# Reordering the chunked linear attention of a streaming-encoder layer, and moving left factors of its feed-forward behind a weight split

## Chip, cores and metric

The kernel runs on one core of a Trainium2 chip (trn2). The metric is the device time in microseconds (us) of one execution, the median of several runs. Beside the times there is one profiled execution, from which the views below are taken.

## What is computed

One layer of a hybrid encoder for 512 frames of width 1024: three parallel branches (gated linear attention over chunks of 64 frames, a causal attention with forget gates, a cross attention into 256 memory tokens), merged by gates, then a squared-ReLU feed-forward. The two places that the change touches are the linear attention and the feed-forward:

```python
def gla_chunk_causal(q, k, v, log_a):        # 4 heads, DK = 64, DV = 128, chunks of 64 frames
    b = cumsum(log_a within the chunk); b_last = b[:, :, -1:]
    q_pos = qc * exp(b)
    a_causal = einsum('bnthd,bnshd->bnhts', q_pos, kc * exp(-b))
    a_anti   = einsum('bnthd,bnshd->bnhts', qc * exp(-b), kc * exp(b))
    attn = where(lower, a_causal, a_anti)
    o_intra = einsum('bnhts,bnshv->bnthv', attn, vc)
    chunk_kv = einsum('bnshd,bnshv->bnhdv', kc * exp(b_last - b), vc)
    prev = scan(state * exp(b_last) + kv)     # the state before each chunk
    o_inter = einsum('bnthd,bnhdv->bnthv', q_pos, prev)
    return o_intra + o_inter
...
    o_gla = rmsnorm(o_gla, g_gla_head) * silu(gg)
...
    h = h + merged @ w_out
    u2 = rmsnorm(h, g_ffn)
    h = h + square(relu(u2 @ w_ff1)) @ w_ff2
    return rmsnorm(h, g_final)
```

## The kernel before

All matrix products with weights run in a split form: an operand is rounded to a high part (`hi`, a cast on ScalarE, ACT) and the rest is its low part (`lo`, a subtraction on VectorE, DVE). `mm3` (L170 to L172) issues three matmuls for one product: high by high and the two mixed ones. `split_w` (L160, L161) and `split_b` (L1331, L1333) make the parts of a weight block of 128 x 1024, `split` (L223, L224) those of an activation. Weight blocks come by DMA into a ring of three buffers, and their high and low parts have rings of three.

The order of the instructions of the TensorE (PE) is the order of the program text. The order of the other engines' instructions is drawn up by a scheduler when the kernel is built; `tc.issue_after(x)` puts what is written under it behind `x` on `x`'s engine, and `in_order()` keeps a stretch of DVE, ACT and SP instructions in the written order.

PSUM holds eight banks in two pools of four: `mmt()` (pool pmm, tiles "mm", used by the products with weights) and `at_()` (pool pa, tiles "a", used by attention, transposes and a part of the products). A tile gets a bank that has been read out.

**Linear attention.** Heads go in two pairs j = 0, 1; 512 frames are handled as four tiles of 128 (two chunks each). The steps of a pair are functions:

- `decays(j)`: cumulative sums of the log decays by matmul (L882), exponentials on ACT (L888, L891), scaled keys and queries `kn`, `qpos`, `kp`, `qneg` on DVE (L896 to L901).
- `key_turn(j)`: three transposes of `kn` (L908) and their copy.
- `gla_scores(j)`: 32 score matmuls (L941), 16 for each of the two masks, the two heads of the pair on the two halves of 64 rows; DVE copies the scores under the mask into `at` (L943), which GpSimd has cleared (L935). At its end it calls `states(j)`: 12 matmuls (L921) into one "mm" tile and the chain of states on DVE (L927, L928).
- `gla_values(j)`: 16 matmuls of scores by values (L952), 12 of queries by states (L956), then the root mean square (square on ACT L962, sum on DVE L963, root on GpSimd L230) and the scaling on DVE (L967).
- `gla_turn(h)`: four transposes (L973) of head h, the product with the gate on DVE (L975) and its split.

`u_sum(n)` are sums on DVE for a later stage, `gate_ready(b)` brings the first weights of that stage. `weave` puts these steps between the units of a filler stream: four projections `gla_g` and four `fox_late` gates, 64 units, each unit one step of the contraction (three matmuls of 512 columns), eight units to one "mm" tile. Each step has a share, and after step i the filler runs up to `units * sum(shares[:i + 1]) // sum(shares)`.

**Feed-forward.** Each of four quarters of the hidden width multiplies by `w_ff1` (first product) and by `w_ff2` (second product), each with seven products of sums of blocks in place of eight. `first_quarter` writes the order of the first quarter out by hand. At its end it issues the second product's parts 1, 2 and 5 (`second`), then the drain of part 2 into the residual (`evac`, L1327), two subtractions (`sub`, L1324) and the left factors of parts 7 (slot 1) and 4 (slot 2) by `left`. `second_product(0)` goes on with parts 3, 6, 7, 4: for each it makes the weight's parts with `split_b` and issues 24 matmuls. Part 3 reads the left factors of slot 0, part 6 those of slot 3.

Of the kernel before, what the change touches and what calls it, by code (L numbers as in the profile page):

```python
# [14 lines left out]
ALU = mybir.AluOpType  # L15
AX = mybir.AxisListType

P = 128
# [4 lines left out]
NT = S // P  # L23
# [40 lines left out]
def hybrid_block(ctx, tc, chunks, wst, memT, xT, xN, gffn, gfin, wup, cst, out):  # L64
    nc = tc.nc
# [5 lines left out]
    def nm(s):  # L71
        uid[0] += 1
        return f"{s}_{uid[0]}"
# [10 lines left out]
    def mmt(shape=None):  # L84
        return pmm.tile(shape or [P, 512], F32, tag="mm", name=nm("mm"))

    def at_(shape=None):
        return pa.tile(shape or [P, 512], F32, tag="a", name=nm("a"))

    def f(ap):  # L90
        return ap.bitcast(F32)
# [77 lines left out]
    def mm3(ps, lh, ll, rh, rl, start, stop, on=False):  # L169
        nc.tensor.matmul(ps, lh, rh, start=start, stop=False, skip_group_check=on)  # L170
        nc.tensor.matmul(ps, lh, rl, start=False, stop=False, skip_group_check=on)  # L171
        nc.tensor.matmul(ps, ll, rh, start=False, stop=stop, skip_group_check=on)  # L172
# [49 lines left out]
    def split(hi, lo, src):  # L222
        nc.scalar.copy(hi, src)  # L223
        return nc.vector.tensor_tensor(lo, src, f(hi), op=ALU.subtract).ins  # L224
# [41 lines left out]
    with pool("front") as fp:  # L266
# [33 lines left out]
        ps = at_()  # L300
# [14 lines left out]
        for j in range(4):  # L315
# [3 lines left out]
            for k in (2 * j, 2 * j + 1):  # L319
# [8 lines left out]
                else:  # L328
                    _, act, vec = parts.send((None, act, vec))
# [98 lines left out]
        ps = at_()  # L428
# [446 lines left out]
    with pool("gla") as lp:  # L875
# [36 lines left out]
        def states(j):  # L912


            dec, kt = gs["d", j][0], gs["k", j]
            mid = gs["s", j] = lp.tile([P, NT, P], F32, tag="mid", name=nm("mid"))
            pv = mmt([P, NT, P])
            for t in range(NT - 1):
                for e in range(2):
                    h = 2 * j + e  # L920
                    nc.tensor.matmul(pv[64 * e:64 * e + 64, t, :], kt[:, t, 64 * e:64 * e + 64], gv[:, t, h * P:(h + 1) * P],  # L921
                                     start=True, stop=True)
            for t in range(NT - 1):
                x = pv[:, t, :]
                if t:
                    x = mid[:, 0, :]
                    nc.vector.tensor_tensor(x, mid[:, t, :], pv[:, t, :], op=ALU.add)  # L927
                nc.vector.tensor_scalar(mid[:, t + 1, :], x, dec[:, t:t + 1], None, op0=ALU.mult)  # L928

        def gla_scores(j):  # L930

            _, kn, kp, qp, qn = gs["d", j]
            ats = gs["a", j] = [lp.tile([P, NT, P], F32, tag=f"at{e}", name=nm("at")) for e in range(2)]
            for at in ats:
                nc.gpsimd.memset(at, 0.0)  # L935
            for m, (kk, qq) in enumerate(((kn, qp), (kp, qn))):
                ps = [at_([P, NT, P]) for _ in range(2)]
                for t in range(NT):
                    sl = slice(t * P, (t + 1) * P)
                    for e in range(2):  # L940
                        nc.tensor.matmul(ps[e][:, t, :], kk[half[e], sl], qq[half[e], sl], start=True, stop=True)  # L941
                for e in range(2):
                    nc.vector.copy_predicated(ats[e], msk_s[:, m:m + 1, :].to_broadcast([P, NT, P]), ps[e])  # L943
            states(j)
# [51 lines left out]
        def gate_ready(b):  # L996
# [3 lines left out]
        A11, A12, A21, A22 = ([f(t[:, 4 * k:4 * k + 4, 256 * i:256 * i + 256]) for t in (uhi, ulo)] for i in range(2) for k in range(2))  # L1000

        steps = (
            (decays, (0,), 13), (key_turn, (0,), 5), (gla_scores, (0,), 8), (gla_values, (0,), 4), (decays, (1,), 5),
            (gla_turn, (0,), 0), (gla_turn, (1,), 4), (key_turn, (1,), 5), (gla_scores, (1,), 2), (u_sum, (1,), 6), (gla_values, (1,), 6),
            (u_sum, (3,), 0), (gla_turn, (2,), 3), (gate_ready, ("11",), 0), (gate_ready, ("21",), 0), (gla_turn, (3,), 3))
        weave([partial(fn, *a) for fn, a, _ in steps], 64, *[gla_g(j) for j in range(4)], fox_late(), shares=[n for *_, n in steps])
    gst.close()
# [24 lines left out]
    with pool("outp") as op_:  # L1032
# [236 lines left out]
        def first_mms(n, w, ps, go=None, low_last=False):  # L1269

            wh, wl = (t.rearrange("p (a k c) -> p a k c", a=2, k=4) for t in w)
            (uh, ul), s = U2[n]

            def mm(a, k, x, y, start, stop):
                nc.tensor.matmul(ps[:, a, :], x[:, a, k, :], y[:, s, k, :], start=start, stop=stop, skip_group_check=go is not None)  # L1275

            for low in range(1 + low_last):
                for a in range(2):
                    for k in range(4):
                        if not low:  # L1280
                            mm(a, k, wh, uh, k == 0 if go is None else go and a == k == 0, False)
                            mm(a, k, wh, ul, False, False)
                        if low or not low_last:
                            mm(a, k, wl, uh, False, k == 3 and (go is None or a == 1))
                        yield
# [9 lines left out]
        rest = first_mms(2, ws[1], banks[0][1], True)  # L1295
# [14 lines left out]
    with pool("ff") as yp:  # L1310
# [12 lines left out]
        def sub(to, x, y, op=ALU.subtract):  # L1323
            return nc.vector.tensor_tensor(to, x, y, op=op).ins  # L1324

        def add(to, x, op=ALU.add):
            return nc.vector.tensor_tensor(to, to, x, op=op).ins  # L1327

        def split_b(raw, after=None):
            hi, lo = (wp.tile([P, 1024], F32R, tag=g, name=nm(g)) for g in ("hi", "lo"))  # L1330
            nc.scalar.copy(hi, raw)  # L1331
            with tc.issue_after(after) if after is not None else ExitStack():
                nc.vector.tensor_tensor(lo, raw, f(hi), op=ALU.subtract)  # L1333
            return hi, lo

        load_n = [0]
# [15 lines left out]
        def left(i, slot, src):  # L1352
            split(ch[i][:, slot, :], cl[i][:, slot, :], src)
# [18 lines left out]
        def first_quarter():  # L1372
# [4 lines left out]
            o12, o22 = ([od[i][:, h, :] for i in range(2)] for h in range(2))  # L1377
# [30 lines left out]
            def left_low(i, slot, src):  # L1408
                nc.vector.tensor_tensor(cl[i][:, slot, :], src, f(ch[i][:, slot, :]), op=ALU.subtract)
# [10 lines left out]
            with tc.issue_after(norm_end[0]), tc.issue_after(norm_end[1]), in_order():  # L1420
# [133 lines left out]
                    second(5, i, five)  # L1554
                for i in range(2):
                    left_low(i, 0, o12[i])
                for t in range(2):
                    evac(0, 2, t, two[t])
                for i in range(2):
                    sub(o21[i], o11[i], o21[i])  # L1560
                    left(i, 1, o21[i])
            for i in range(2):
                left(i, 2, o22[i])

        def first_evac(n, i, ps):

# [37 lines left out]
        def evac(q, n, t, ps):  # L1604
            if n in (1, 2):
                add(C(0, 0, t), ps)
            if n == 3:
                add(C(0, 1, t), ps)
            if n == 6:
                add(C(0, 1, t), ps, ALU.subtract)  # L1610
                if q == 0:
                    nc.scalar.copy(R7[t], ps)
                else:
                    add(R7[t], ps)
            if n == 7:
                add(R7[t], ps)
            if n == 4:
                add(C(1, 0, t), ps)
# [19 lines left out]
        def second_mms(q, n, js, ps, w, ts=range(2), cols=slice(0, 512), fresh=None):  # L1638

            keep, on = n in (1, 5), q == NQ - 1 and n in CHAIN  # L1640
            first, end = fresh or (not (keep and q or on), not keep or q == NQ - 1)
            for t in ts:
                for i in js:
                    for k in range(2):
                        sl = slice(256 * k + t * P, 256 * k + t * P + P)
                        mm3(ps[t], ch[i][:, LEFT[n], sl], cl[i][:, LEFT[n], sl], w[i][0][:, k, cols], w[i][1][:, k, cols],
                            i == k == 0 and first, i == k == 1 and end, on and fresh is None)
                if q < NQ - 1 and js[-1] == 1 and not keep and (q or n != 2):
                    evac(q, n, t, ps[t])

        def second_product(q):
            for n in SECOND[0 if q else 3:]:
                ps = held[n] if n in (1, 5) else [mmt() for _ in range(2)]
                for i in range(2):
                    w = {i: [x.rearrange("p (k c) -> p k c", k=2) for x in split_b(factor_raw(q, n, i))]}
                    second_mms(q, n, [i], ps, w)
                for i in range(2):
                    if n == 1:
                        add(od[i][:, 0, :], s1[i])
                        left(i, 0, od[i][:, 0, :])  # L1660
                    if n == 2:
                        sub(ev[i][:, 1, :], ev[i][:, 0, :], ev[i][:, 1, :])
                        left(i, 1, ev[i][:, 1, :])
                    if n == 5:
                        left(i, 2, od[i][:, 1, :])

        def last_product():
# [64 lines left out]
            with in_order():  # L1732
# [115 lines left out]
                scale_r(2, 1, nc.sync)  # L1848
                scale_r(3, 1, nc.scalar)
                scale(3, 0, nc.sync, 256)  # L1850
        first_quarter()
        second_product(0)
        for q in range(1, NQ):
            first_product(q, 0)
            loads = load_blocks(q)
# [113 lines left out]
```

## Time and profile before

| | |
|---|---|
| median of 3 runs | 809.85 us (809.58 to 811.93) |
| profiled execution | 809.57 us |
| its span, first to last instruction | 807.8 us |
| PE busy | 798.7 us (99%) |
| DVE, ACT, GpSimd (POOL) busy | 595.6, 445.7, 108.0 us |
| mean granted TensorE clock | 0.997 |
| DMA | 161.29 MB, mean 200 GB/s |

Times in the views count from the start of the span. PE is the matmuls, PEld the weight loads that run beside them. In the timeline a row is start, duration, engine, line, operation, output<-inputs, shapes and count; equal neighbours are merged. In the chain a row is start, duration and the piece of work. The linear attention lies between 254 and 316 us, the part of the feed-forward that the change moves between 527 and 566 us.

### The profile page before, as it was taken

What the parts mean: (1) busy time and instruction counts of PE and PEld (TensorE: products, weight loads), DVE (VectorE), ACT (ScalarE), POOL (GpSimd) and SP (SyncE); (2) the same over time, 40 slices, a digit from 0 to 9 for tenths busy, and PEclk for the clock granted to TensorE, in tenths of its full rate; (3) what the DMA queues carried; (4) which work ended last, traced back from release to release, by engine and by line L of the source; (5) the groups of instructions that cost most, each with busy time, mean ns of one, the idle gap of its engine ahead of it and who ended that gap; (6) DMA issues with size and microseconds to landing.
All of it is one profiled execution on the core that took longest, in us unless ns stands there. A gap on an engine that the chain in (4) does not pass through costs nothing.

```text
span 807.8 us, 12486 instructions
## 1 busy us (share of the span) xinstructions
PE 798.7 (99%) x4799; PEld 704.8 (87%) x4799; DVE 595.6 (74%) x917; ACT 445.7 (55%) x702; POOL 108.0 (13%) x136
## 2 busy tenths in 40 slices
PE   9999999999999999999999999999999999999996
PEld 7788888888888888999999889988998899889985
DVE  6878877456465687877567558797788778887897
ACT  7867555443344234444354446874676377647764
POOL 0001010101101111143144100011001100100011
PEclk9999999999999999999999999999999999999998
DMA  9354665788787867757758823898758966896644
GB/s 356 140 162 160 196 164 182 209 239 241 212 262 244 235 209 196 184 143 207 199 142 234 271 70 131 287 258 211 234 169 197 225 210 168 193 269 202 166 84 129
DMA packets 39628, 161.29 MB, mean 200 GB/s; under 512 B 4752, under 2 KB 5456, under 8 KB 37200
## 3 DMA queue, kind: packets, MB, share of 16 engines
q1 hardware_dynamic: 28432, 98.34, 34.6%
q0 software_dynamic: 9776, 58.20, 34.0%
q10 hardware_dynamic: 1360, 3.96, 1.5%
q8 instruction: 37, 0.61, 0.3%
q14 instruction: 23, 0.19, 0.1%
HBM read 158.35 MB, written 35.68 MB: 240 GB/s over the span
## 4 chain that ended last, share of the span: by engine, by line
PE 98%; DMA 0%; ACT 0%; DVE 0%; POOLq 0%; issue 0%; DVEq 0%; POOL 0%; ACTq 0%
PE mm L1275 20%; PE mm L170 17%; PE mm L171 16%; PE mm L172 16%; PE a L170 6%; PE a L171 6%; PE a L172 6%; PE mm L391 1%; PE a L404 1%; PE mm L611 1%; PE a L664 1%; PE a L702 1%; PE a L701 1%; PE a L941 1%; DMA mem_s<-in_memT_dram 0%; PE mm L620 0%
## 5 line engine op out<-in xcount | busy, mean ns | idle before, releaser
L161 DVE TENSOR_TENSOR wlo<-raw,whi 128x1024 fp32r<-128x1024 f32 x61 | 79.6, 1306 | 56.5 <-ACT whi L160 56.3
L170 PE MATMUL mm<-uhi,whi 128*128 128x512 f32 (+1 forms) x336 | 119.7, 356 | 0.0
L172 PE MATMUL mm<-uhi,wlo 128*128 128x512 f32 (+1 forms) x336 | 117.5, 350 | 0.0
L171 PE MATMUL mm<-ulo,whi 128*128 128x512 f32 (+1 forms) x336 | 117.3, 349 | 0.0
L160 ACT CAST whi<-raw 128x1024 fp32r<-128x1024 f32 x61 | 64.3, 1054 | 87.6 <-PE mm L171 47.0
L1331 ACT CAST hi<-raw 128x1024 fp32r<-128x1024 f32 x52 | 54.6, 1052 | 41.6 <-PE mm L1275 29.5
L1333 DVE TENSOR_TENSOR lo<-raw,hi 128x1024 fp32r<-128x1024 f32 x52 | 63.4, 1223 | 15.6 <-ACT hi L1331 15.6
L170 PEld LDWEIGHTS mm<-uhi,whi 128*128 128x128 f32 x336 | 63.7, 190 | 9.3 <-issue 1.5
L172 PEld LDWEIGHTS mm<-uhi,wlo 128*128 128x128 f32 x336 | 63.6, 189 | 8.5
L171 PEld LDWEIGHTS mm<-ulo,whi 128*128 128x128 f32 x336 | 63.7, 189 | 7.5
L1275 PE MATMUL mm<-u2l,hi 128*128 128x256 f32 x240 | 66.1, 283 | 0.0
L1275 PE MATMUL mm<-u2h,hi 128*128 128x256 f32 x240 | 66.1, 283 | 0.0
L1275 PE MATMUL mm<-u2h,lo 128*128 128x256 f32 x240 | 61.1, 283 | 0.0
L1635 POOL DMA_DIRECT2D b<-in_wst_dram x30 | 25.6, 854 | 262.2 <-DVE lo L1333 134.1
L1275 PE MATMUL mm<-u2sh,hi 128*128 128x256 f32 x192 | 52.6, 283 | 0.0
L1275 PE MATMUL mm<-u2sl,hi 128*128 128x256 f32 x192 | 52.5, 283 | 0.0
L170 PE MATMUL mm<-hi,ch 128*128 128x512 f32 (+1 forms) x132 | 50.9, 386 | 0.0
L171 PE MATMUL mm<-lo,ch 128*128 128x512 f32 (+1 forms) x132 | 50.9, 386 | 0.0
L172 PE MATMUL mm<-hi,cl 128*128 128x512 f32 (+1 forms) x132 | 50.9, 386 | 0.0
L1275 PE MATMUL mm<-u2sh,lo 128*128 128x256 f32 x192 | 47.5, 283 | 0.0
L1275 PEld LDWEIGHTS mm<-u2h,hi 128*128 128x128 f32 x240 | 46.1, 192 | 0.1
L1275 PEld LDWEIGHTS mm<-u2l,hi 128*128 128x128 f32 x240 | 46.1, 192 | 0.1
(446 smaller groups left out, 2143.7 us busy)
## 6 DMA issues: line engine op xcount, KB each, us to landing
raw<-in_wst_dram SPq DMA_DIRECT2D x113, 512.0 KB
raw<-T SPq DMA_DIRECT2D x32, 512.0 KB
b<-in_wst_dram POOLq DMA_DIRECT2D x32, 512.0 KB, 5.6
T<-in_wst_dram POOLq DMA_DIRECT2D x12, 1024.0 KB, 8.9
b<-in_wst_dram SPq DMA_DIRECT2D x16, 512.0 KB
wb<-in_wst_dram POOLq DMA_DIRECT2D x15, 512.0 KB, 5.4
T<-in_wst_dram POOLq DMA_DIRECT2D x12, 512.0 KB, 5.7
wb<-in_wst_dram SPq DMA_DIRECT2D x8, 512.0 KB
```

Source lines behind the costliest of these rows:

```text
L160: cast = nc.scalar.copy(hi, raw)
L161: low_now[0] = nc.vector.tensor_tensor(lo, raw, f(hi), op=ALU.subtract).ins
L170: nc.tensor.matmul(ps, lh, rh, start=start, stop=False, skip_group_check=on)
L171: nc.tensor.matmul(ps, lh, rl, start=False, stop=False, skip_group_check=on)
L172: nc.tensor.matmul(ps, ll, rh, start=False, stop=stop, skip_group_check=on)
L391: nc.tensor.matmul(kps[h], w[:, h * P:(h + 1) * P], x[:, k, :], start=k == p == 0, stop=k == KT - 1 and p == 2)
L404: nc.tensor.matmul(ps, x[:, k, sl], w[low][:, kk, :], start=k == low == 0 and x is mxh, stop=k == KT - 1 and low == 1)
L611: nc.tensor.matmul(ps, w[0][:, k, :], u[:, k, :], start=k == 0 and u is uhi, stop=False)
L1275: nc.tensor.matmul(ps[:, a, :], x[:, a, k, :], y[:, s, k, :], start=start, stop=stop, skip_group_check=go is not None)
L1331: nc.scalar.copy(hi, raw)
L1333: nc.vector.tensor_tensor(lo, raw, f(hi), op=ALU.subtract)
L1635: nc.gpsimd.dma_start(to[i], wst[index["B", q, i, x]], accum_op=ALU.add)
```

## The change

In the linear attention the steps are put in another order: the decays and the key turn of the second pair come before the first pair's values, the scores and states of the second pair follow directly on the first pair's values with no filler between, and the turns of heads 0 and 1 come after them. The shares are new. The second mask's scores of the second pair go to two "mm" tiles in place of two "a" tiles.

In the feed-forward `split_b` records its last cast and subtraction. The end of `first_quarter` (drain of part 2, subtractions, left factors of slots 1 and 2) becomes a function `rest`, which `second_product(0)` calls after the matmuls of part 3, behind the cast (on ACT) and the subtraction (on DVE) of part 3's second weight block.

```diff
             for m, (kk, qq) in enumerate(((kn, qp), (kp, qn))):
-                ps = [at_([P, NT, P]) for _ in range(2)]
+                ps = [(mmt if j and m else at_)([P, NT, P]) for _ in range(2)]
...
         steps = (
-            (decays, (0,), 13), (key_turn, (0,), 5), (gla_scores, (0,), 8), (gla_values, (0,), 4), (decays, (1,), 5),
-            (gla_turn, (0,), 0), (gla_turn, (1,), 4), (key_turn, (1,), 5), (gla_scores, (1,), 2), (u_sum, (1,), 6), (gla_values, (1,), 6),
+            (decays, (0,), 13), (key_turn, (0,), 5), (gla_scores, (0,), 2), (decays, (1,), 9), (key_turn, (1,), 4),
+            (gla_values, (0,), 0), (gla_scores, (1,), 8), (gla_turn, (0,), 0), (gla_turn, (1,), 2), (u_sum, (1,), 4), (gla_values, (1,), 8),
             (u_sum, (3,), 0), (gla_turn, (2,), 3), (gate_ready, ("11",), 0), (gate_ready, ("21",), 0), (gla_turn, (3,), 3))
...
-        def split_b(raw, after=None):
+        split_now = [None, None]
+
+        def split_b(raw):
             hi, lo = (wp.tile([P, 1024], F32R, tag=g, name=nm(g)) for g in ("hi", "lo"))
-            nc.scalar.copy(hi, raw)
-            with tc.issue_after(after) if after is not None else ExitStack():
-                nc.vector.tensor_tensor(lo, raw, f(hi), op=ALU.subtract)
+            split_now[0] = nc.scalar.copy(hi, raw).ins
+            split_now[1] = nc.vector.tensor_tensor(lo, raw, f(hi), op=ALU.subtract).ins
             return hi, lo
...
+            def rest():
+
                 for t in range(2):
                     evac(0, 2, t, two[t])
                 for i in range(2):
                     sub(o21[i], o11[i], o21[i])
                     left(i, 1, o21[i])
-            for i in range(2):
-                left(i, 2, o22[i])
+                for i in range(2):
+                    left(i, 2, o22[i])
+            return rest
...
-        def second_product(q):
+        def second_product(q, rest=None):
...
                     second_mms(q, n, [i], ps, w)
+                if n == 3 and rest is not None:
+                    with tc.issue_after(split_now[0]), tc.issue_after(split_now[1]):
+                        rest()
...
-        first_quarter()
-        second_product(0)
+        second_product(0, first_quarter())
```

## The prediction

> **What bounds the kernel now.** I read the page's busy times and chain first, then the waits of the TensorE, then the chain and the timeline piece by piece where the change cuts in.
>
> ```profile
> span 807.8 us, 12486 instructions
> PE 798.7 (99%) x4799; PEld 704.8 (87%) x4799; DVE 595.6 (74%) x917; ACT 445.7 (55%) x702; POOL 108.0 (13%) x136
> ...
> PE 98%; DMA 0%; ACT 0%; DVE 0%; POOLq 0%; issue 0%; DVEq 0%; POOL 0%; ACTq 0%
> ```
> ```profile
> PE a L302 <- DVE warm L299: 1.2, 1, 1.2
> PE mm L391 <- ACT hi L286: 0.8, 1, 0.8
> ```
> ```profile
> 280.00:300.00 20.00, 20.00 (x128) 16.63 (x127) 16.75 (x36) 6.62 (x12) 3.57 (x5) 1.00 0.74 237
> 540.00:560.00 20.00, 20.00 (x90) 16.57 (x89) 17.58 (x23) 10.88 (x14) 2.55 (x3) 1.00 0.87 220
> ```
>
> PE is 98% of the chain. Its two waits add up to 2.0 us and belong to the first lines of the kernel, far from the change. In the two stretches that the change rewrites (columns: PE, PEld, DVE, ACT, POOL busy, clock, DMA share, GB/s) PE is busy for all 20 us at a granted clock of 1.00. So nothing visible is left to win. But a 512-column matmul is drawn 0.39 us long while the next one starts 0.23 us later, so a wait under some 0.16 us vanishes under the drawn end. I therefore read starts, not busy time: each start later than the usual step is time lost on the path.
>
> **Part 1, the order of the linear attention.** Work of the pairs lies between units of a filler stream (three 512-column matmuls, 3 x 0.23 = 0.69 us a unit, 64 units). I call the steps of pair 0 and 1 decays D, key turn K, scores with states S, values V. From the two share lists, as 64 x running sum / total, V0 stood alone after unit 26 and S1 after unit 44; now V0 and S1 stand together after unit 34, with the output turns of heads 0 and 1 after unit 43 and V1 after unit 49 (52 before).
>
> ```profile
> 267.75 0.39 PE L172 MATMUL mm<-uhi,wlo 128*128 128x512 f32 x1
> 268.07 1.16 PE L941 MATMUL a<-qpos,kn 64*128 64x128 f32 x16
> ...
> 278.30 0.94 PE L956 MATMUL a<-mid,qpos 64*128 64x128 f32 x12
> 279.17 0.50 PE L170 MATMUL mm<-uhi,whi 128*128 128x512 f32 x1
> 279.51 0.40 PE L171 MATMUL mm<-ulo,whi 128*128 128x512 f32 x1
> 279.74 0.40 PE L172 MATMUL mm<-uhi,wlo 128*128 128x512 f32 x1
> ...
> 293.83 1.16 PE L941 MATMUL a<-qpos,kn 64*128 64x128 f32 x16
> 294.83 1.47 PE L941 MATMUL a<-qneg,kp 64*128 64x128 f32 x16
> 296.23 0.88 PE L921 MATMUL mm<-gv,kt 128*64 128x128 f32 x12
> ```
> ```profile
> 268.14 1.99 PE a L941 x32
> 270.12 0.81 PE mm L921 x12
> 276.59 1.78 PE a L952 x16
> 278.37 0.87 PE a L956 x12
> 293.90 2.40 PE a L941 x32
> 309.76 0.44 PE a L973 x4
> 312.29 0.85 PE a L973 x4
> ```
>
> (a) *One border fewer.* The scores L941 and the end of the values L956 use 64 rows, two matmuls at a time. With p for a pair and d for the change of shape at either end, 16p + 2d = 1.99 and 6p + 2d = 0.87, so p = 0.112 and d = 0.10. When V0's end meets S1's start, two d go (0.20). The last stream matmul before a group steps 268.07 - 267.75 = 0.32 instead of 0.23 (0.09 goes), and the first one behind steps 279.51 - 279.17 = 0.34 (0.11 goes). Sum: -0.40 us, with no unknown but the joint itself, which the trace of before does not hold. Bounds: -0.40, and 0 if the two groups still change over as they do now; I take -0.40, because both sides have the same 64 rows.
>
> The Trainium skill, page "TensorEngine Tiling (Array Packing)", Key Properties, says that a change of tiling mode, not of tile alone, drains the TensorE. It has no figure for that; the rows above do (0.10 at each end), and by the rule as by the rows the joint costs nothing, since the mode stays.
>
> (b) *The second mask's banks.* S0's 32 score matmuls take 1.99, S1's 2.40: 0.41 more, and it lies in the second mask (294.83 to 296.23 = 1.40, the first mask 293.83 to 294.83 = 1.00). What ends there is a read of the same four-bank pool by the DVE:
>
> ```profile
> 294.40 0.68 DVE L975 TENSOR_TENSOR og<-a,sg 128x512 f32<-128x512 f32 x1
> ```
>
> That is the gate product on a turned head's bank, ending at 295.08, inside the stretch that is too long. In the change this mask gets banks of the other pool, and the turns come after S1. -0.41 us; bounds -0.41 and +0.2 (a new wait on the other pool of half that size).
>
> (c) *The last turn.* The turns of heads 2 and 3 are the same four transposes, 0.44 and 0.85. The second waits, quarter by quarter, for
>
> ```profile
> 311.64 1.11 DVE L967 TENSOR_SCALAR on<-a,rr 128x128 f32<-128x128 f32 x4
> ```
>
> From V1's start to the turn of head 3 there are now 11 units, 9 before: 1.4 us more room for a wait of 0.41. I book -0.30, since the DVE's order is drawn up anew; bounds -0.41 and 0.
>
> (d) *What is pulled forward.* D1 comes 10 units before K1 (5 before, with T0 and T1 between). K1 needs kn:
>
> ```profile
> 282.05 1.05 PE L882 MATMUL a<-cst_s,la 128*128 128x128 f32 x8
> ...
> 287.12 0.68 DVE L896 TENSOR_TENSOR kn<-gkT,ex 128x512 f32<-128x512 f32 x1
> ...
> 288.92 0.68 DVE L901 TENSOR_TENSOR qneg<-gqT,ex 128x512 f32<-128x512 f32 x1
> ```
>
> From D1 to kn's end 5.75 us, to qneg's end 7.55. K1 now starts 0.9 + 10 x 0.69 = 7.8 after D1, S1 another 0.4 + 4 x 0.69 + 2.65 = 5.8 later. Both are covered, by 2 and 6 us, though S0's mask copies lie ahead on DVE. Cost 0; without the cover up to 1 us for K1.
>
> Part 1 sums to -0.40 - 0.41 - 0.30 = -1.1 us.
>
> **Part 2, the left factors behind the split.** In the feed-forward's first quarter the drain of product 2, two subtractions and four left factors now wait on ACT and DVE for both splits of product 3. No DMA and no matmul moves.
>
> ```profile
> 541.33 1.05 ACT L1331 CAST hi<-raw 128x1024 fp32r<-128x1024 f32 x1
> ```
> ```profile
> 539.44 1.23 DVE L1333 TENSOR_TENSOR lo<-raw,hi 128x1024 fp32r<-128x1024 f32 x1
> ...
> 541.78 1.28 DVE L1327 TENSOR_TENSOR h<-h,mm 128x512 f32<-128x512 f32 x2
> ...
> 544.18 1.22 DVE L1333 TENSOR_TENSOR lo<-raw,hi 128x1024 fp32r<-128x1024 f32 x1
> ...
> 545.92 1.22 DVE L1333 TENSOR_TENSOR lo<-b,hi 128x1024 fp32r<-128x1024 f32 x1
> ```
> ```profile
> 543.55 0.39 PE L170 MATMUL mm<-hi,ch 128*128 128x512 f32 x1
> ...
> 548.99 0.39 PE L170 MATMUL mm<-hi,ch 128*128 128x512 f32 x1
> ```
>
> Product 3 starts at 543.55; its second half (12 matmuls later, 546.3) needs the low part that ends at 545.40. So this split has 0.9 us to spare already, and its coming earlier (behind the cast, 542.4 to 543.6) buys nothing. What now queues behind it: the drain of product 2 (DVE) would end near 544.9 instead of 543.06, and product 6 needs that bank at 548.99; product 6's first low part ends at 547.14 and is due at 549.2, 2.1 us of cover against a delay of about 0.5 (542.0 to 542.4, idle while the cast runs, plus a shifted place). If all the moved DVE work (1.28 and six operations of about 0.6, near 4.9) ran ahead of that low part, it would end at 543.6 + 4.9 + 1.2 = 549.7 and PE would wait 0.5. Bounds 0 and +0.5; I take 0. Together the change is worth -1.1 us on this profile.
>
> **Rivals.** *R1, the banks of the other pool run out (slower).* After S1, three of its four banks (two masks, states) are taken and the filler's current product holds the fourth. The next product begins 6 units after S1, at V0's start + 2.65 + 2.6 + 4.1 = 9.4 us, and needs a bank that DVE has read out. For it:
>
> ```profile
> 269.98 2.58 DVE L943 COPY_PREDICATED at<-msk_s,a 128x512 f32<-128x512 uint8 x4
> ...
> 284.27 1.12 DVE L967 TENSOR_SCALAR on<-a,rr 128x128 f32<-128x128 f32 x4
> 285.38 1.23 DVE L161 TENSOR_TENSOR wlo<-raw,whi 128x1024 fp32r<-128x1024 f32 x1
> ```
>
> V0 began at 276.59 in the chain and its normalisation left DVE at 285.39, 8.8 after. If the mask copies queue behind all that, the third copy frees a bank at 8.8 + 3 x 0.65 = 10.75, 1.35 late, and 2.6 late with a weight's low part between. It decides as soon as the third copy ends later than 9.4. Time: 1.35 to 2.6 less the 1.1 gained, so 809.8 to 811.1; I name 810.8. Against it: that chain has DVE gaps (ACT's squares, POOL's roots) in which the copies fit. The Trainium skill, page "Perfetto Trace Analysis", section Matmuls, asks that independent matmul groups rotate through different banks so that one's evacuation runs under the next; read against the change, taking three of the filler's four banks is this rival. No row of before shows it.
>
> *R2, the gain is eaten downstream (no change).* The gate products behind this stage already wait once:
>
> ```profile
> 337.65 0.28 PE L170 MATMUL mm<-f2h,whi 128*128 128x256 f32 x1
> 337.92 0.39 PE L171 MATMUL mm<-f2l,whi 128*128 128x256 f32 x1
> ```
>
> The step is 0.27 instead of the 0.12 of 256 columns. If what they wait for does not move forward with PE, the 1.1 comes back here: 809.6. Against: that chain begins with the end of the filler on PE, so most of it moves along.
>
> *R3, the change does less than it says*: the joint keeps its drains and the last turn still waits, so only (b) is won: 809.2.
>
> **How the numbers follow.** The profiled execution took 809.57 us (span 807.8 and 1.8 around it), the lowest of the runs; the median of the three is 809.85. So 809.57 - 1.1 = 808.5; for a median I add 0.1 of their 0.28: 808.6. Chances: forecast 0.60, R1 0.20, R2 0.10, R3 0.10. Low end: every term at its best, -1.22, and 0.7 for what lies hidden in pairs of matmuls that I cannot see: 807.6. High end: R1's 811.1 and 0.3 of part 2's bound of 0.5: 811.4. A measurement here tells about 0.3% (2.4 us) from no change. The terms that could be won are 1.2 us in all, so faster by over 0.3% gets only 0.06, for a mechanism I have not seen; slower by over 0.3% needs R1 and part 2 and more to fall together: 0.11. Within: 0.83.
>
> **What would show it.** Right: one piece of the chain with L956 directly followed by L941, no lengthened stream step between; S1's scores in about 1.9 us; the turn of head 3 at 0.44; PE without waits near 545 to 555. Wrong: a PE wait on DVE L943 or L928 at the filler's start behind S1 (R1); the step at the f2h/f2l product grown by about a microsecond (R2); a PE wait on DVE L1333 or on the drain L1327 in the feed-forward (part 2). A time below 807.6 or above 811.4 would mean that the order drawn up for ACT and DVE changed elsewhere.

## The result and the profile after

The changed kernel takes 808.74 us (median of 22 runs, 808.18 to 813.48); the kernel before took 810.01 beside it. The ratio is 0.9988 [0.9982, 0.9993], so the gain is 1.0 us, between 0.6 and 1.5 (the medians lie 1.27 apart). The profiled execution took 808.35 us, 1.22 less than the 809.57 of before.

The totals on the profile page of the kernel after:

```profile
span 806.6 us, 12488 instructions
PE 797.8 (99%) x4799; PEld 704.6 (87%) x4799; DVE 596.0 (74%) x917; ACT 445.3 (55%) x702; POOL 107.3 (13%) x136
```

Its waits of the TensorE, and its windows over the two stretches that were rewritten (columns as in the prediction):

```profile
PE a L302 <- DVE warm L299: 1.2, 1, 1.2
PE mm L391 <- ACT hi L286: 0.5, 1, 0.5
```
```profile
280.00:300.00 20.00, 20.00 (x144) 17.14 (x143) 14.21 (x31) 6.71 (x10) 4.47 (x6) 1.00 0.78 238
540.00:560.00 20.00, 20.00 (x90) 16.54 (x90) 17.51 (x24) 11.48 (x14) 3.34 (x4) 1.00 0.84 216
```

Nothing in these views tells that a microsecond was won. PE was full before and is full now. The gain is seen only where starts are compared at the same piece of work. Two pieces serve as marks: the first cumulative sums of the linear attention (L882), and the first transposes of the feed-forward's input (L1260). First the chain of before, then the chain of after with the pieces of the change between the marks:

```profile
254.62 0.89 PE a L882 x8
...
478.01 0.87 PE a L1260 x8
```
```profile
254.63 0.89 PE a L882 x8
...
283.31 1.78 PE a L952 x16
285.09 0.87 PE a L956 x12
285.96 0.89 PE a L941 x16
286.86 0.89 PE mm L941 x16
287.75 0.81 PE mm L921 x12
...
310.79 0.44 PE a L973 x4
...
476.80 0.87 PE a L1260 x8
```

Both kernels reach the first mark at the same time. (The experiments below reach it between 254.47 and 255.28 us, though the program text ahead of it is the same in all; so a difference between the two marks says more than a difference of two times.) The second mark comes at 476.80 instead of 478.01: 1.22 us between the marks (223.39 to 222.17), which is all of the difference. The feed-forward adds nothing: the start of part 3 of the second product moved from 543.55 to

```profile
542.31 0.39 PE L170 MATMUL mm<-hi,ch 128*128 128x512 f32 x1
```

that is by 1.24. In the chain the values of the first pair (L956) are followed directly by the second pair's scores (L941); the second mask's 16 matmuls (output "mm") take as long as the first's, 0.89; and the turn of head 3 (the last L973) takes 0.44.

### The profile page after: what moved, and what is told of

It is laid out like the page before. It is cut to its first block, busy times and chain, and to the rows that moved or that the text cites. A ratio compares the mean times of both kernels' runs of the same rounds, so it can differ in the third digit from the quotient of the medians.

```text
span 806.6 us, 12488 instructions
## 1 busy us (share of the span) xinstructions
PE 797.8 (99%) x4799; PEld 704.6 (87%) x4799; DVE 596.0 (74%) x917; ACT 445.3 (55%) x702; POOL 107.3 (13%) x136
## 4 chain that ended last, share of the span: by engine, by line
PE 98%; DMA 0%; ACT 0%; DVE 0%; POOLq 0%; issue 0%; DVEq 0%; POOL 0%; ACTq 0%
PE mm L1275 20%; PE mm L170 17%; PE mm L172 17%; PE mm L171 16%; PE a L170 6%; PE a L171 6%; PE a L172 6%; PE mm L391 1%; PE a L404 1%; PE mm L611 1%; PE a L664 1%; PE a L702 1%; PE a L701 1%; DMA mem_s<-in_memT_dram 0%; PE mm L620 0%; PE a L952 0%
## 5 line engine op out<-in xcount | busy, mean ns | idle before, releaser
L171 PE MATMUL mm<-ulo,whi 128*128 128x512 f32 (+1 forms) x336 | 117.3, 349 | 0.0
L171 PEld LDWEIGHTS mm<-ulo,whi 128*128 128x128 f32 x336 | 63.7, 190 | 7.5
L171 PE MATMUL mm<-lo,ch 128*128 128x512 f32 (+1 forms) x132 | 50.9, 386 | 0.0
```

## The experiments

Each was compared with the kernel before, on the same chip. The kernel before had medians of 809.82 to 809.97 in these comparisons.

**The two parts apart.** The first kernel is the one before with the new order, shares and banks of the linear attention alone; the second is the changed kernel with the old attention, so only the left factors move.

```diff
# e1: before, with
-                ps = [at_([P, NT, P]) for _ in range(2)]
+                ps = [(mmt if j and m else at_)([P, NT, P]) for _ in range(2)]
...  (and the new steps)
# e2: after, with this line and the steps as before
```

> Only the attention's new order, shares and banks; the feed-forward as before. Theory (the gain is three pieces of PE time in the attention: a border 0.40, S1's second mask 0.41, the last turn 0.41): 1.2 us less than before, ratio 0.9985, span about 806.6, and the three pieces in the chain as in the changed kernel. Rival (the split carries part of the gain): less than 0.8 us gained.

> Only the feed-forward's rest behind the split; the attention as before. Theory: no PE wait lay there, so the ratio is 1.000 (within 0.0005) and PE steps from 527 to 566 us stay at 0.23. Rival: a gain of 0.4 us or more, or a PE wait of up to 0.5 us at part 6's first low part.

The attention alone: 808.74 us, ratio 0.9991 [0.9982, 1.0], profiled 808.6. The left factors alone: 809.87, ratio 0.9999 [0.999, 1.0008]. The chain of the second one still has the long scores of the second pair and the long last turn:

```profile
293.79 2.39 PE a L941 x32
...
312.19 0.85 PE a L973 x4
```

Between the marks the attention alone takes 222.16 us, as the whole change does, and the left factors alone take 223.43, as the kernel before does. All of the gain belongs to the attention; none shows for part 2.

**The banks without the order.** The kernel before with the line on `ps` alone.

```diff
-                ps = [at_([P, NT, P]) for _ in range(2)]
+                ps = [(mmt if j and m else at_)([P, NT, P]) for _ in range(2)]
```

> The old order of steps, with only the second pair's second mask in the other pool; feed-forward as before. Theory: S1's 32 scores take 1.99 instead of 2.40 us, the rest is as before: 0.4 us less than before, ratio 0.9995. Rival (the long scores are no bank wait but a property of that place): 2.40 stays and the ratio is 1.000.

809.21 us, ratio 0.9992 [0.9983, 1.0001]: by the times only a direction. Its chain decides:

```profile
294.21 1.09 PE a L941 x16
295.30 0.89 PE mm L941 x16
```

The two masks take 1.98 instead of 2.40, so term (b) is 0.42 (0.39 between the marks) and comes from the banks alone. The execution profiled was itself no faster than before (809.81). It reached the first mark 0.31 late (254.93), and it lost as much again in the feed-forward; this second loss led to the last experiments. In its timeline of PE the second half of part 3 lacks its low part:

```profile
546.16 0.39 PE L170 MATMUL mm<-hi,ch 128*128 128x512 f32 x1
546.59 0.50 PE L171 MATMUL mm<-lo,ch 128*128 128x512 f32 x1
```

The step is 0.43 instead of 0.23, and the next one 0.34. The timeline of ACT, of this run and of before, shows why:

```profile
537.75 1.05 ACT L1386 CAST hi<-b 128x1024 fp32r<-128x1024 f32 x1 [1.83 <-DMA b<-in_wst_dram]
```
```profile
536.15 1.05 ACT L1386 CAST hi<-b 128x1024 fp32r<-128x1024 f32 x1
```

The cast of a block of weights waited for its DMA and began 1.6 us later than in the profile of before, with the same feed-forward program. So the old order of part 2 has little to spare in part 3's split, and in this execution a late block used it up.

**The order without the banks.** The changed kernel with the second mask back in the "a" pool.

```diff
-                ps = [(mmt if j and m else at_)([P, NT, P]) for _ in range(2)]
+                ps = [at_([P, NT, P]) for _ in range(2)]
```

> The changed kernel with the second mask's scores back in the four-bank attention pool. Theory: of its four banks two hold the first mask and two hold V0's output, which DVE read out 7.1 and 10.6 us after V0's start in the changed kernel, while the mask wants them 3.5 us after it: PE waits 3.5 us for the first and 5 to 7 us in all, 813.5 to 816 us. Rival (the order alone makes the gain, the banks are a trifle): 808.7 to 809.2 us.

811.54 us, ratio 1.0021 [1.0009, 1.0032], profiled 812.56 (the ten executions lie between 810.32 and 814.15). Slower, as expected, but by less than I wrote. The timeline of PE:

```profile
286.26 1.06 PE L941 MATMUL a<-qpos,kn 64*128 64x128 f32 x16
288.67 2.18 PE L941 MATMUL a<-qneg,kp 64*128 64x128 f32 x16 [1.35 <-DVE at L943]
...
292.26 0.80 PE L170 MATMUL mm<-uhi,whi 128*128 128x512 f32 x1
```

I had expected the second mask to wait for the banks of the first pair's values. It waited for the first mask's own banks instead, which the copies L943 empty earlier. From the start of the scores to the next stream matmul it is 6.0 us; in the changed kernel it is 2.68 (285.80 to 288.48, shown below). Only a part of that is the wait of 1.35. The windows of the same kernel:

```profile
287.00:289.00 2.00, 0.65 (x8) 0.42 (x6) 1.88 (x4) 0.65 (x2) 0.94 (x1) 1.00 1.03 221
289.00:291.00 2.00, 1.88 (x18) 1.50 (x18) 2.00 (x8) 0.00 (x0) 0.11 (x2) 0.71 0.93 229
291.00:293.00 2.00, 2.00 (x14) 1.57 (x13) 2.00 (x6) 0.00 (x0) 0.99 (x1) 0.50 0.99 401
293.00:295.00 2.00, 2.00 (x10) 1.60 (x9) 1.56 (x6) 0.00 (x0) 0.00 (x0) 0.94 0.66 270
```

After the pause the granted clock falls to 0.50, and most of the second mask and the states run at half speed. So the banks are not an extra beside the new order. Without them the new order is 1.7 us slower than the kernel before.

**One unit back into the joint.** The changed kernel with one filler unit between the first pair's values and the second pair's scores. In this and the following diffs of steps the shares add up to 64, so that each is a number of filler units; the lines with a minus are the changed kernel's steps in these units.

```diff
-            (gla_scores, (0,), 2), (decays, (1,), 10), (key_turn, (1,), 4), (gla_values, (0,), 0), (gla_scores, (1,), 9),
+            (gla_scores, (0,), 2), (decays, (1,), 10), (key_turn, (1,), 3), (gla_values, (0,), 1), (gla_scores, (1,), 9),
```

> The changed kernel with one filler unit of the four ahead of V0 moved to between V0 and S1; all else in its place. Theory: the border comes back with its two changes of shape and two lengthened stream steps: 0.40 us more than the changed kernel, S1's 32 scores 1.99 instead of 1.78 us, V0's end 0.87, the steps ahead of S1 0.32 and behind V0 0.34. Rival (the joint is worth nothing by itself): same steps as in the changed kernel, 0.

809.19 us, ratio 0.9987 [0.9977, 0.9997]. The runs do not separate 0.4 us from the changed kernel; the chain does:

```profile
284.55 0.87 PE a L956 x12
...
286.32 1.09 PE a L941 x16
287.41 0.89 PE mm L941 x16
```

The scores are back at 1.98, where the joint gives 1.78. Compare the timeline of PE of the changed kernel:

```profile
285.02 0.94 PE L956 MATMUL a<-mid,qpos 64*128 64x128 f32 x12
285.80 1.06 PE L941 MATMUL a<-qpos,kn 64*128 64x128 f32 x16
...
288.48 0.50 PE L170 MATMUL mm<-uhi,whi 128*128 128x512 f32 x1
288.82 0.39 PE L171 MATMUL mm<-ulo,whi 128*128 128x512 f32 x1
```

Here only one lengthened stream step (0.34) is left, behind the whole group; with the unit between there are two more (0.34 at 285.35 and 0.33 at 285.92 in its timeline). Shape changes and steps together make the joint worth 0.41; between the marks this kernel takes 222.61, 0.44 more than the changed kernel.

**The second pair's values two units later.** The changed kernel with 9 units, instead of 11, between these values and the turn of head 3.

```diff
-            (u_sum, (1,), 4), (gla_values, (1,), 8),
+            (u_sum, (1,), 6), (gla_values, (1,), 6),
```

> The changed kernel with V1 two units later, so that it is 9 units ahead of head 3's turn as before the change. Theory: the turn of head 3 waits again for its scaling on DVE: 0.85 instead of 0.44 us, 0.4 us more than the changed kernel. Rival (the wait went because DVE's queue is shorter in the new order): 0.44 stays.

809.55 us, ratio 0.9996 [0.9987, 1.0005]. The timeline of PE has the wait of the kernel before again, and more of it:

```profile
310.77 0.40 PE L172 MATMUL mm<-uhi,wlo 128*128 128x512 f32 x1
311.67 1.02 PE L973 MATMUL a<-cst_s,on 128*128 128x128 f32 x4 [0.51 <-DVE on L967]
```

The step before the turn is 0.90 instead of 0.23, and the turn itself takes 0.78 (to the next stream matmul at 312.45) instead of 0.36: 1.1 us lost, where I expected 0.41. Between the marks it is 1.07 (223.24 for 222.17). The timeline of DVE, of this kernel and then of the changed one, shows what the turn waits for:

```profile
311.19 1.12 DVE L967 TENSOR_SCALAR on<-a,rr 128x128 f32<-128x128 f32 x4
```
```profile
307.72 1.13 DVE L967 TENSOR_SCALAR on<-a,rr 128x128 f32<-128x128 f32 x4 [1.19 <-POOL rr L230]
```

Here, as in the kernel before, the scaling stands behind a weight's low part, a gate product and a sum; in the changed kernel the scheduler drew it ahead of all three. It ends 10.8 us after the second pair's values start (301.49), and the turn is due after 9.5; in the changed kernel it ends after 9.1. With that place in DVE's order 9 units would have covered it, by an estimate from these rows. So moving the values changed two things, the room and the place of L967 in the queue, and this experiment does not separate them.

**The group next to the filler's border.** The changed kernel with the first pair's values and the second pair's scores five units later, one unit before the filler needs its next "mm" bank.

```diff
-            (key_turn, (1,), 4), (gla_values, (0,), 0), (gla_scores, (1,), 9), ..., (u_sum, (1,), 4), (gla_values, (1,), 8),
+            (key_turn, (1,), 9), (gla_values, (0,), 0), (gla_scores, (1,), 9), ..., (u_sum, (1,), 0), (gla_values, (1,), 7),
```

> The changed kernel with V0 and S1 five units later, one unit ahead of the filler's next product instead of six. Theory (three of the four banks are taken by S1, the fourth by the filler): that product starts 6.0 us after V0, and DVE has read out the third copy's bank 7.7 us after V0 in the changed kernel, so PE waits 1.6 us there: 1.6 us more than the changed kernel, 810.3 us. Rival (a bank is free, or the copies are drawn ahead): no wait, 808.7 us.

810.44 us, ratio 1.0007 [0.9998, 1.0016], profiled 810.28. Its waits:

```profile
PE mm L170 <- DVE at L943: 1.6, 1, 1.6
```

The wait of 1.6 us is what was expected, and the time too. The third copy ends 7.7 us after the values begin (294.60 for 286.90), as in the changed kernel. Rival R1 is a real mechanism. The change escapes it by its place, six units ahead of the border. In the changed kernel the same copies stand in the timeline of DVE as

```profile
287.42 1.35 DVE L943 COPY_PREDICATED at<-msk_s,a 128x512 f32<-128x512 uint8 x2
...
290.29 1.35 DVE L943 COPY_PREDICATED at<-msk_s,mm 128x512 f32<-128x512 uint8 x2
```

The third copy (the first of the later two) ends near 290.97, which is 7.7 us after the values began at 283.31. The deadline was 9.4 by the prediction's sum, so 1.7 us are to spare.

**More joints.** The idea carried on: the key turn, the scores of the first pair and the decays of the second in a row, the key turn of the second pair directly before the first pair's values, the turns of heads 0 and 1 directly before the second pair's values, the last two turns together, and both pairs' second masks on "mm" banks.

```diff
-                ps = [(mmt if j and m else at_)([P, NT, P]) for _ in range(2)]
+                ps = [(mmt if m else at_)([P, NT, P]) for _ in range(2)]
...
+            (decays, (0,), 18), (key_turn, (0,), 0), (gla_scores, (0,), 0), (decays, (1,), 16), (key_turn, (1,), 0), (gla_values, (0,), 0),
+            (gla_scores, (1,), 10), (u_sum, (1,), 4), (gla_turn, (0,), 0), (gla_turn, (1,), 0), (gla_values, (1,), 10),
+            (u_sum, (3,), 2), ..., (gla_turn, (2,), 0), (gla_turn, (3,), 4)
```

> The changed kernel with five more borders joined: key turn, scores and states of pair 0 and decays of pair 1 in a row; key turn of pair 1, V0 and S1 in a row; turns of heads 0 and 1 and V1 in a row; turns of heads 2 and 3 in a row; the first pair's second mask on the other pool too. Theory: each border saves one lengthened stream step of 0.09 to 0.11 us: 0.45 us less than the changed kernel, if no new wait appears. Rival (bursts without filler make PE wait for ACT and DVE): waits of 0.5 us or more at the groups L921, L941 or L973.

808.52 us, ratio 0.9984 [0.9975, 0.9992], profiled 807.96. This is the best median, but its interval overlaps that of the change. Between the first decays and the first transposes of the feed-forward's input it takes 0.22 us less than the changed kernel, where I expected 0.45. Its chain shows one reason:

```profile
270.74 1.09 PE a L882 x8
```

The decays take 0.89 when they stand alone, and 1.09 directly behind the states (L921, to 270.74). Here, setting groups of different shapes side by side removed lengthened stream steps but not the change of shape.

**Later sums of weights.** The theory from the third experiment: in the old order a late block stops PE in part 3's second half; in the new order the left factors stand behind that split, and the same lateness stops PE in part 6 instead. To make a block late, the DMA of the first quarter that adds block 12 onto block 11, for part 5 of the second product, was cut into shorter pieces, first for both weight blocks, then for the second alone; each once without and once with part 2 of the change (both with the new attention).

```diff
-                    nc.gpsimd.dma_start(b11[i], wst[index["B", 0, i, "12"]], accum_op=ALU.add)
+                    nc.gpsimd.dma_start(b11[i], wst[index["B", 0, i, "12"]], accum_op=ALU.add, max_dma_last_dim=256)
# then:                                                      max_dma_last_dim=512 if i else None
```

> The attention's change alone, with the two DMAs that add block 12 onto block 11 for part 5 of the first quarter cut into shorter pieces, so that they land later while the order of all other engines stays. Theory: the casts and low parts of part 5 come later by the delay d, the queue behind them shifts, and part 3's second low part, which has 1.05 us to spare here, makes PE wait d - 1.05 at the second half of part 3 (the wait of 0.3 us that the old order with new banks showed there). For d under 1 us no wait. Rival (that wait had another cause): a late sum makes no wait in part 3.

> The whole change with the same cut DMAs. Theory A (the moved factors only move the margin): part 3's second low part now has 3.1 us to spare, but part 6's first low part only 1.1 instead of 2.1, so PE waits about as long as in the kernel without the move, at part 6 instead of part 3. Theory B (the move is a cover against late sums): no wait in part 3 or 6, and the time is lower than without the move by the wait there.

813.4 us without part 2 (ratio 1.0046 [1.003, 1.0062]) and 813.82 with it (1.0043 [1.0029, 1.0057]). This pair tells nothing about the theory: the block was so late that part 5, ahead of part 3, waited for its high part in both. The waits without and with part 2:

```profile
PE a L170 <- ACT hi L1386: 1.2, 1, 1.2
```
```profile
PE a L170 <- ACT hi L1387: 2.7, 1, 2.7
```

With a smaller delay:

> The attention's change alone, and of the two adding DMAs only the second one cut into shorter pieces, so that only part 5's second half comes late, by some 3 us, and barely in time for PE. Theory: the DVE queue behind it shifts by 2.5 to 3 us; part 3's second low part, with 1.05 us to spare, makes PE wait 1.5 to 2 us at the second half of part 3. Rival: no wait in part 3.

> The whole change with the same single cut DMA. Theory A (the move shifts the margin from one split to the next): no wait in part 3, whose low part has 3.1 us to spare, but 1.5 to 2 us at part 6's first low part, which has 1.1 to spare; the same time as without the move. Theory B (the move is a cover against late sums): no wait in either, 1.5 to 2 us less than without the move.

811.04 us without (1.0014 [1.0005, 1.0022]) and 811.27 with part 2 (1.002 [1.0011, 1.0028]). The timeline of PE without part 2, in part 3's second half, and then with it, in part 6:

```profile
545.64 0.39 PE L170 MATMUL mm<-hi,ch 128*128 128x512 f32 x1
546.76 0.50 PE L171 MATMUL mm<-lo,ch 128*128 128x512 f32 x1 [0.74 <-DVE lo L1333]
```
```profile
549.56 0.39 PE L170 MATMUL mm<-hi,ch 128*128 128x512 f32 x1
550.30 0.50 PE L171 MATMUL mm<-lo,ch 128*128 128x512 f32 x1 [0.35 <-DVE lo L1334]
```

The steps are 1.12 and 0.74 instead of 0.23. With the lengthened steps near them, and for part 6 a second short wait at 553.23, the losses are 1.0 and 0.8 us, where I had written 1.5 to 2. In these two executions the wait changes its place as theory A says, and it costs about the same. Both kernels also waited in part 5 (0.5 and 1.1 us), so the two medians do not compare part 2 cleanly; whether it can pay when a block is late stays open.

## Why the prediction was right

The forecast was 808.6 us; 808.74 was measured. The profiled difference was forecast as -1.1 and is -1.22, the sum of the terms' best bounds. That the median came within 0.14 is partly luck: the gain was 0.12 larger than the sum, and the median of after lies 0.39 above its profiled execution, where 0.1 was added; the two errors have opposite signs.

- *(a), the joint, -0.40.* 0.41: the values' end and the scores take 0.87 + 1.78 = 2.65 where the two apart take 0.87 + 1.99 (0.21), and two lengthened steps are gone (0.09 and 0.11). The one open point, whether the joint itself costs a change of shape, is settled by the experiment with one unit between. The Trainium skill, page "TensorEngine Tiling (Array Packing)", Key Properties, says that changing the tiling mode drains the TensorE and changing the tile alone does not; these rows agree, with 0.10 at each end of a group. The row of the decays behind the states (1.09 for 0.89) shows the other half of it: where the shape changes at a joint, the 0.20 stay.
- *(b), the second mask's banks, -0.41.* 0.42 by the rows, 0.39 between the marks, from the banks alone.
- *(c), the last turn.* This term was mis-sized: booked at -0.30, it measured -0.41, its bound. I held back 0.11 because DVE's order could have moved against it. The order moved in its favour. In the kernel before, the scaling of head 3 ends 10.1 us after the second pair's values start (302.61 to 312.75); the turn now comes 10.9 after (299.75 to 310.62), so the room alone would have covered it, by an estimate from these rows. But the scaling also moved forward on DVE and ends after 9.1 (308.85), which the sum did not foresee. In the experiment with 9 units it stood behind other work again, and the loss became 1.1.
- *(d), the steps pulled forward, 0.* Right. The keys `kn` of the second pair are ready 4 us before their turn at 280.23, twice the cover that I had worked out:

```profile
275.39 0.69 DVE L896 TENSOR_TENSOR kn<-gkT,ex 128x512 f32<-128x512 f32 x1 [0.90 <-POOL ex L893]
```

- *Part 2, 0.* The cost is right, the delay was not: I took 0.5 us for part 6's first low part. The timeline of DVE after:

```profile
540.92 1.23 DVE L1334 TENSOR_TENSOR lo<-raw,hi 128x1024 fp32r<-128x1024 f32 x1 [0.15 <-ACT hi L1333]
...
545.66 1.22 DVE L1334 TENSOR_TENSOR lo<-b,hi 128x1024 fp32r<-128x1024 f32 x1
```

It starts at 545.66 against 545.92 before. PE's work moved 1.22 forward and this only 0.26, so it is about 1.0 late, and its cover fell from 2.1 to 1.1 us. Part 3's second low part now ends at 542.15. Counted to the first matmul that reads it (L171 of the second half, at 546.49 before and 545.25 after), its spare time grew from 1.1 to 3.1; the 0.9 of the prediction counted to the matmul ahead of that one. So the shortest cover, 1.1 us, went from part 3 to part 6 with the same size. Nothing waited there in the kernel before, so nothing was won; with a late block the wait moved along with the short cover.
- *R1* would have needed the third copy 1.7 us later; with the group next to the border it comes true. *R3* is refuted: the joint pays and the last turn no longer waits. *R2* is refuted by the step at the gate products, in the timeline of PE after:

```profile
336.45 0.28 PE L170 MATMUL mm<-f2h,whi 128*128 128x256 f32 x1
336.70 0.39 PE L171 MATMUL mm<-f2l,whi 128*128 128x256 f32 x1
```

It is 0.25, was 0.27, and stands 1.2 us earlier: the chain behind it moved along with PE.

## What to carry to other kernels

Where the matmul engine looks full, read the starts of its matmuls, not its busy time: the 1.22 us lay in three pieces of about 0.41 under drawn ends. Put groups of the same array shape next to each other, and give such a longer burst banks from a second pool, but well ahead of the moment when the stream next needs one of them. Moving work behind a split moved the spare time here from one deadline to the next; look at what the new neighbour has left before calling it a gain.

## What was not expected of the hardware

A short pause of the TensorE can cost more than its length. After the pause of 1.35 us in the kernel with the old banks the clock was 0.50 for (0.29 x 2 + 0.50 x 2 + 0.06 x 2) / 0.5 = 3.4 us. After waits of 0.55, 1.17 and 0.76 us in the first kernel with late sums (ending at 537.85, 541.80 and 543.06) it fell as well:

```profile
540.00:544.00 4.00, 2.07 (x8) 1.16 (x7) 2.21 (x3) 2.87 (x4) 0.70 (x1) 0.98 0.68 123
544.00:548.00 4.00, 4.00 (x13) 3.14 (x12) 4.00 (x7) 2.62 (x5) 0.16 (x1) 0.60 0.80 133
```

That is (0.02 x 4 + 0.40 x 4) / 0.5 = 3.4 us again. In the kernel with both sums late and part 2, after a wait of 2.7 us, the clocks of 0.91, 0.50 and 0.74 in the three windows of 4 us from 540 on give (0.09 x 4 + 0.50 x 4 + 0.26 x 4) / 0.5 = 6.8 us, twice that. Yet behind the wait of 1.6 us at the filler's border the clock stayed at 1.00, and so it did behind the waits of 0.7 to 0.8 us in the last pair of kernels. The Trainium skill, page "TensorE: Matmul & The Clock Gate", section "What's actually happening", describes a free-running window of about 3.4 us and a half clock after at least one idle window. The length of 3.4 us agrees; but here a pause of 1.35 us, well short of a window, was enough, and one of 1.6 us was not. That the place of a pause within the window decides would fit these cases, and no run here tests it.

A DMA's landing differed between two profiled executions by more than a microsecond. The cast of one block, which reads what a DMA brings, began at 536.15 in the profile of before and at 537.75 in the kernel with only the banks changed, where it waited for the landing; the DMA was issued at 529.65 and 529.54.
